# A trunk of three layers on one core: the second block's experts without a branch each, weights by slots, a Newton step on each reciprocal root

## The chip, the cores and the metric

One core of one Trainium2 chip runs the whole program. The metric is the device time of an execution in microseconds, the median of the runs. All data are 32-bit floats.

## The reference

The input is 256 tokens of 1024 features (x), and further 256 context tokens. Three layers follow each other. Each has a mixer over the tokens and a mixture of 16 experts, both behind a root-mean-square norm with a scale, a shift and a gate from a conditioning vector (adaLN).

```python
def first_block(...):                       # layers 0 and 1
    h = rms_norm(x, mix_norm_g[l]) * (1 + scale) + shift
    y = fourier_conv_mixer(h, ...) if l % 2 == 0 else windowed_attention(h, ...)
    x = x + gate * y
    h = rms_norm(x, ffn_norm_g[l]) * (1 + scale) + shift
    x = x + gate * ec_moe(h, router_w[l], ..., moe_w_gate[l], moe_w_up[l], moe_w_down[l])
```

In the first block the experts choose: each of the 16 takes the 32 tokens with the highest affinity, and has three matrices of 1024 x 1024 (gate, up, down). In the second block (layer 2) the tokens choose: of four groups of experts the best one, and in it the best two experts. An expert can get any number of tokens from 0 to 256; the mean is 32. Its matrices are w1 and w3 (1024 x 512) and w2 (512 x 1024), y = (silu(h w1) * (h w3)) w2, weighted by the token's gates. A last root-mean-square norm ends the program.

## The kernel before

**Weights.** All weights pass through a ring of 14 slots of 1 MB (`ring`, 128 partitions x 2048 floats). The list `order` says which slot holds what and in what order; class `Stream` asks for the next slot (L281, on SyncE's queue) as soon as a slot is freed in the program. Its order is adaLN weights, projections and experts as the layers need them: each expert of the first block is 12 slots (four each of gate, up, down), each of the second block 6 (two each of w1, w3, w2; 96 in all). A slot of a matrix is taken from the matrix as it lies in memory: `kview` puts row k * 128 + p on partition p, so a slot of gate, up, down or w2 is two runs of 4 KB in each partition, one of w1, w3 or a projection by columns (`by_cols`) four runs of 2 KB. The scale and shift part of an adaLN matrix is one run of 8 KB (of rows of 12 KB, or 24 KB in the second block), and a few tables (taps, transforms, pooling, `wb`) are laid out without gaps by the host.

**First block's experts** (`moe_ec`, matmuls of L1015): after the routing, expert by expert, gate, up and down on 32 tokens, with the results of four experts scattered back together (L1056).

**Second block's experts** (`moe2`): after the router, `rank` holds each token's place among its expert's tokens, `gates` its weights and `cnt` the number of tokens of each expert. `take` gathers the first 64 tokens of a pair of experts by a one-hot matmul (L1724) and prepares the way back (`sT`, L1739). `mlp` is one expert in steps: w1 and w3 (L1753, result in bank u), silu on ScalarE (L1758), the product `hid` on VectorE (L1762), its transposes (L1767), w2 (L1777) and the gated result Y (L1781). `scatter` adds a pair's Y back into x (L1685, L1686). Steps of two experts are interleaved. After w3 of every expert `more` (L1784) reads the expert's count into a register of TensorE, ScalarE and VectorE (L1786) and branches (L1787): with over 64 tokens the expert's weights are used again for slots 64 to 95 (`block`, matmuls on 32 tokens), with over 96 (L1797) and over 128 (L1799) for more. Only then are w1 and w3 freed. With the last scatter go the sums of squares for the last norm (L585) and the product with its weights (L1690).

**Roots.** `rstd` (L603 to L606) and three other places take a square root on ScalarE and a reciprocal on VectorE.

The order of instructions on each engine is made by a scheduling layer from the program's order and its own estimates of durations; a branch is a border that it moves little over.

Of the kernel before, what the change touches and what calls it, by code (L numbers as in the profile page):

```python
# [12 lines left out]
I32 = mybir.dt.int32  # L13
# [17 lines left out]
RING = 14  # L31


# ---------------------------------------------------------------- constants (shapes alone)
class Pack:
    """Columns of a [128, n] array, by name."""
# [95 lines left out]
def filter_consts():  # L132
    """Tables for the long filters."""
# [16 lines left out]
def tap_pack(i):  # L150
    """Tables for the spectrum of the 31 taps, the taps, and the bias of the convolution."""
# [15 lines left out]
def filter_pack(i):  # L167
    """Parameters of the long filters."""
# [19 lines left out]
def pool_consts():  # L188
    """Mean of a window less the middle, by the size of the window."""
# [63 lines left out]
# ---------------------------------------------------------------- the kernel  # L253
class Parts:
    """Feature tiles kept two by two, indexed as one [128, 2 * n, tokens]."""
# [8 lines left out]
class Stream:  # L264
    """Slots of weights, loaded in one order ahead of their use; parts of a slot lie side by side."""
# [6 lines left out]
    def pump(self):  # L272
        while self.issued < len(self.order) and self.issued - len(self.freed) < RING:
            key, parts = self.order[self.issued]
            t = self.pool.tile([128, SLOT], F32, name="w")
            v, at = t[:, :sum(int(np.prod(ap.shape[1:])) for ap in parts)], 0
            if len(parts[0].shape) == 3:
                v = v.rearrange("p (a b) -> p a b", a=parts[0].shape[1])
# [22 lines left out]
def weave(*gens):  # L301
    """Steps of several pieces of work in turn, each as (generator, steps at a time)."""
# [17 lines left out]
def trunk_kernel(ctx: ExitStack, tc: tile.TileContext, I: dict, O: dict):  # L320
# [16 lines left out]
    # ---- what stays  # L337
# [20 lines left out]
    def kview(ap, k0, k1):  # L358
        return ap[k0 * 128:k1 * 128].rearrange("(k p) n -> p k n", p=128)
# [1579 lines left out]
```

## Time and profile before

| | |
|---|---|
| median of the runs | 1871.93 us (3 runs, 1869.08 to 1872.28) |
| span of the profiled execution, first to last instruction | 1864.1 us |
| TensorE (matmul) busy | 1460.4 us, 78% |
| VectorE, ScalarE, GpSimd busy | 438.2, 238.4, 10.3 us |
| read from memory | 627.09 MB, 337 GB/s over the span |
| blocks for an expert's tokens past 64 that ran | 1 (L1753 with xgx: 128 records, two for a matmul, 64 matmuls a block) |

The runs are timed without the profile; the profiled execution's own time is its span. PE is TensorE, PEld its weight loads, DVE VectorE, ACT ScalarE, SP SyncE; a q behind a name is the engine's sequencer. PEclk is the share of TensorE's 2.4 GHz that was granted. A 32-bit matmul leaves two records. The DMA share is the mean busy share of the 16 DMA engines.

### The profile page before, as it was taken

The numbers are of one execution on the slowest core, as the hardware profiler recorded it, in microseconds if no ns is written. First come the engines' busy times: TensorE is split into PE (matmuls) and PEld (weight loads), VectorE is DVE, ScalarE is ACT, GpSimd is POOL, SyncE is SP. The second block draws the span as 40 slices with busy tenths as digits, with TensorE's granted clock in tenths as the row PEclk, the third lists the DMA queues.
The fourth block names the chain that finished last, engine by engine and source line by source line (L and its number), as shares of the span: only waits on it lengthen the run. The fifth ranks groups of instructions, "written<-read, shape, count | busy, mean of one in ns | idle before, by whom it ended". The sixth has DMA issues, their size and how long they took to land. (4 is left out here: it accounts for less than half of the span.)

```text
span 1864.1 us, 25272 instructions
## 1 busy us (share of the span) xinstructions
PE 1460.4 (78%) x10913; PEld 742.4 (40%) x10913; DVE 438.2 (24%) x981; ACT 238.4 (13%) x550; POOL 10.3 (1%) x19
## 2 busy tenths in 40 slices
PE   6997778767666699986676766677999978788887
PEld 2444324223222246452232322244767545445442
DVE  2513113110010057231110101101333241222123
ACT  2022002000000014221000000001222120001011
POOL 0000000000000000000000000000000000000000
PEclk9998868776676699996866866889989989999998
DMA  9987999999999998399999999999713748889770
GB/s 364 411 309 306 410 409 409 409 409 409 409 409 409 406 389 320 114 407 409 409 409 409 409 409 409 409 404 394 282 46 136 265 161 313 304 333 342 283 262 24
DMA packets 180860, 630.30 MB, mean 338 GB/s; under 512 B 10880, under 2 KB 13056, under 8 KB 174048
## 3 DMA queue, kind: packets, MB, share of 16 engines
q1 hardware_dynamic: 178464, 624.38, 86.1%
q0 software_dynamic: 1952, 3.16, 0.6%
q8 instruction: 117, 1.92, 0.4%
q10 hardware_dynamic: 288, 0.52, 0.1%
q14 instruction: 39, 0.32, 0.0%
HBM read 627.09 MB, written 1.05 MB: 337 GB/s over the span
## 5 line engine op out<-in xcount | busy, mean ns | idle before, releaser
L1015 PE MATMUL b<-w,xg 128*32 128x256 f32 x4096 | 361.6, 496 | 183.0 <-DMA w<-in_moe_w_up_dram 110.0
L1015 PEld LDWEIGHTS b<-w,xg 128*32 128x32 f32 x4096 | 136.3, 132 | 404.6 <-DMA w<-in_moe_w_up_dram 161.8
L1015 PE MATMUL b<-w,hidT 128*32 128x256 f32 x2048 | 185.5, 505 | 63.7 <-DMA w<-in_moe_w_down_dram 47.5
L1753 PE MATMUL u<-w,xg 128*64 128x256 f32 x1024 | 130.9, 399 | 14.7 <-PEq L1787 14.0
L1015 PEld LDWEIGHTS b<-w,hidT 128*32 128x32 f32 x2048 | 68.4, 135 | 165.3 <-DMA w<-in_moe_w_down_dram 88.3
L1035 DVE TENSOR_TENSOR hid<-b,sg 128x256 f32<-128x256 f32 x32 | 13.6, 425 | 512.6 <-PE b L1015 417.8
L1043 DVE SCALAR_TENSOR_TENSOR Y<-b,cc,gq 32x256 f32<-32x256 f32 x128 | 61.5, 481 | 223.9 <-PE b L1015 222.4
L1753 PEld LDWEIGHTS u<-w,xg 128*64 128x64 f32 x1024 | 82.0, 143 | 58.2 <-issue 29.8
L1777 PE MATMUL b<-w,hidT 128*64 128x512 f32 x256 | 73.5, 701 | 37.1 <-PEq L1787 33.2
L1030 ACT ACTIVATE sg<-b 128x256 f32<-128x256 f32 x32 | 12.3, 384 | 436.8 <-PE b L1015 436.7
L1777 PEld LDWEIGHTS b<-w,hidT 128*64 128x64 f32 x256 | 24.6, 161 | 76.8 <-issue 75.2
L1040 ACT COPY hidT<-b 128x256 f32<-128x256 f32 x32 | 11.9, 372 | 323.8 <-PE b L1038 323.8
L1056 PE MATMUL b<-Y,gT 128*128 128x512 f32 x64 | 39.1, 762 | 9.5 <-DVE Y L1043 9.5
L784 PE MATMUL b<-w,hT 128*128 128x512 f32 x96 | 43.3, 612 | 1.1 <-DVE hT L633 1.1
L461 DVE SCALAR_TENSOR_TENSOR w<-w,cond 128x1024 f32<-128x1024 f32 x35 | 43.5, 1277 | 1.2 <-DMA w<-in_ada_w_dram 1.1
L1137 PE MATMUL b<-w,hT 128*128 128x512 f32 x96 | 42.2, 594 | 0.0
L1762 DVE TENSOR_TENSOR hid<-u,sg 128x256 f32<-128x256 f32 x16 | 6.8, 425 | 147.9 <-PEq L1787 86.1
L952 PE MATMUL b<-oh,n 128*128 128x128 f32 x256 | 39.4, 320 | 0.9 <-DVE oh L995 0.9
L952 PEld LDWEIGHTS b<-oh,n 128*128 128x128 f32 x256 | 36.9, 231 | 7.5 <-issue 6.1
L1287 PE MATMUL b<-pe,w 128*128 128x256 f32 x160 | 38.6, 396 | 0.0
L1781 DVE TENSOR_TENSOR Y<-b,hkb 64x512 f32<-64x512 f32 x32 | 22.0, 689 | 67.7 <-PE b L1777 67.5
L1728 ACT ACTIVATE xg<-b,shsc 128x128 f32<-128x128 f32 x32 | 14.6, 460 | 158.5 <-DVE xg L1731 158.5
(445 smaller groups left out, 1484.7 us busy)
## 6 DMA issues: line engine op xcount, KB each, us to landing
w<-in_moe_w_gate_dram SPq DMA_DIRECT2D x128, 1024.0 KB, 18.5
w<-in_moe_w_up_dram SPq DMA_DIRECT2D x128, 1024.0 KB, 18.6
w<-in_moe_w_down_dram SPq DMA_DIRECT2D x128, 1024.0 KB, 18.5
w<-in_moe_w_dram SPq DMA_DIRECT2D x96, 1024.0 KB, 10.3
w<-in_ada_w_dram SPq DMA_DIRECT2D x72, 1024.0 KB, 13.1
w<-in_w_in_dram SPq DMA_DIRECT2D x8, 1024.0 KB, 16.6
w<-in_fc_w_in_dram SPq DMA_DIRECT2D x6, 1024.0 KB, 20.4
w<-in_attn_w_qkv_dram SPq DMA_DIRECT2D x6, 1024.0 KB, 16.1
```

The source lines that it names most:

```text
L461: V.scalar_tensor_tensor(into[:, hs], w[:, hs], c, into[:, hs], op0=OP.mult, op1=OP.add)
L784: T.matmul(p, hT[:, kt, b * 128:(b + 1) * 128], w(kt), start=kt == 0, stop=kt == 7)
L952: T.matmul(p[:, j * 128:(j + 1) * 128], n[:, b, dt * 128:(dt + 1) * 128], oh[:, b, g * 128:(g + 1) * 128], start=b == 0, stop=b == 1)
L1015: T.matmul(p[32 * q:32 * q + 32, :256], lhs(kt), w[:, k, q * 256:(q + 1) * 256], start=kt == 0, stop=kt == 7)
L1043: V.scalar_tensor_tensor(Y[32 * j:32 * j + 32, q * 256:(q + 1) * 256], pd[32 * q:32 * q + 32, :256], cc[32 * q:32 * q + 32, e:e + 1], gq[3 ...
L1056: T.matmul(p, gT[:, b * 128:(b + 1) * 128], Y[:, h * 512:(h + 1) * 512], start=True, stop=True)
L1137: T.matmul(p, hT[:, kt, b * 128:(b + 1) * 128], w(kt), start=kt == 0, stop=kt == 7)
L1287: T.matmul(p[:, j * 256:(j + 1) * 256], w(kt)[:, c0 + j * 128:c0 + (j + 1) * 128], h[:, kt], start=kt == 0, stop=kt == 7)
L1728: A.activation(xg[:, dt, :m], p[:, j * 128:j * 128 + m], AF.Identity, bias=shsc[:, 0, dt:dt + 1], scale=shsc[:, 1, dt:dt + 1])
L1753: T.matmul(p[rows[h], :nu], xg[:, kt, c], w(kt)[:, h * nu:(h + 1) * nu], start=kt == 0, stop=kt == 7)
L1777: T.matmul(pd[rows[h], :nd], hidT[:, kt % nj, rows[kt // nj]], w(kt)[:, h * nd:(h + 1) * nd], start=kt == 0, stop=kt == 3)
L1781: V.tensor_tensor(Y[c, h * nd:(h + 1) * nd], pd[rows[h], :nd], gq2[rows[h], at:at + nd], op=OP.mult)
```

## The change

1. **Layout.** The host cuts every matrix into slots (`weight_slots`): what goes into a slot lies in memory partition after partition, 8 KB each, and `Stream` loads it as one flat [128, 2048]. The bytes, the slots and their order stay.
2. **Second block.** `more` and its branches go. Every expert takes its first 64 tokens, and w1, w3 and w2 are freed right behind their last matmul. Tokens past 64 become jobs of 64 tokens: a list of at most seven (`keys`, `top`, `je`, `jk`, `ji`) is made on VectorE behind the routing, and behind the last pair's scatter a nest of branches runs as many jobs as there are, each with its expert's six slots loaded again on SyncE's queue from an address in a register, and its own gather, matmuls and scatter. The sums of the last norm stand behind the jobs.
3. **Roots.** After sqrt and reciprocal one Newton step, three small VectorE operations (`inv_root`), at all places.

Comments and docstrings are gone as well, so line numbers differ.

```diff
+def by_rows(w, per):
+    *lead, k, n = w.shape
+    w = w.reshape(*lead, k // (128 * per), per, 128, n)
+    return np.ascontiguousarray(np.swapaxes(w, -3, -2))
...
     def pump(self):
         while self.issued < len(self.order) and self.issued - len(self.freed) < RING:
-            key, parts = self.order[self.issued]
+            key, ap = self.order[self.issued]
             t = self.pool.tile([128, SLOT], F32, name="w")
...
-            for ap in parts:
-                n = ap.shape[-1]
-                self.nc.sync.dma_start(v[..., at:at + n], ap)
-                at += n
+            flat = ap.rearrange("p a b -> p (a b)") if len(ap.shape) == 3 else ap
+            v = t[:, :flat.shape[1]]
+            self.nc.sync.dma_start(v, flat)
...
+    def inv_root(m, n=2):
+        r = small.tile([128, 8], F32, name="root")[:, :n]
+        t = small.tile([128, 8], F32, name="step", bufs=1)[:, :n]
+        A.activation(r, m, AF.Sqrt)
+        V.reciprocal(r, r)
+        V.scalar_tensor_tensor(t, r, -0.5, r, op0=OP.mult, op1=OP.mult)
+        V.tensor_tensor(t, t, m, op=OP.mult)
+        V.scalar_tensor_tensor(r, t, 1.5, r, op0=OP.add, op1=OP.mult)
+        return r
...
-            def more(e, hid):
-                c = nc.values_load(cnt[0:1, e:e + 1], engines=ENGINES, min_val=0, max_val=256)
-                with tc.If(c > 64):
...
-                    block(64, 32)
-                    with tc.If(c > 96):
-                        block(96, 32)
-                        with tc.If(c > 128):
-                            block(128, 64)
-                            block(192, 64)
+            for k in range(3):
+                V.scalar_tensor_tensor(keys[:, k], cnt, 64.5 + 64 * k, cv("iota_r")[:, 256 - 48 + 16 * k:256 - 32 + 16 * k], op0=OP.is_gt, op1=OP.mult)
+            V.max(top, keys.rearrange("p k e -> p (k e)"))
+            V.tensor_scalar(at, top, 0.0, None, op0=OP.is_gt)
+            V.tensor_reduce(jk[:, 0:1], at, axis=AX.X, op=OP.add)
+            V.tensor_copy(ji[:, 8:9], jk[0:1, 0:1])
...
+            def job(j):
+                e = nc.values_load(ji[0:1, j:j + 1], engines=(mybir.EngineType.SP,), min_val=0, max_val=15, ...)
+                def load(nm):
+                    v = I[f"moe_{nm}_2"].rearrange("e i p k n -> p e i (k n)")
...
+                        nc.sync.dma_start(t, v[:, bass.ds(e, 1), i].rearrange("p e n -> p (e n)"))
...
+                take([(rs[:, 0], rs[:, 1])], t)
+                run(mlp(None, t["xg"], 0, t["Y"], lambda nm: ws[nm]))
+                scatter(t["sT"], t["Y"], 64)
+            def jobs(j=0):
+                if j == JOBS:
+                    return
+                with tc.If(n_jobs > j):
+                    job(j)
+                    jobs(j + 1)
...
-            scatter(t["sT"], t["Y"], 128, True)
+            scatter(t["sT"], t["Y"], 128)
+            jobs()
+            for b in range(2):
+                for h in range(2):
+                    hs = slice(h * 512, (h + 1) * 512)
+                    sums(ssf, b, h, x)
+                    (V if b else G).tensor_tensor(n[:, b, hs], x[:, b, hs], fg[:, hs], op=OP.mult)
             r = rstd(ssf)
```

The order of TensorE's instructions shows the second part. Before, from the branch behind expert 1's w3 to the one behind expert 2's; w1 and w3 of an expert are L1753, w2 L1777, the gather L1724, names with an x at the end belong to the block past 64 tokens:

```order
L1787 UNCONDITIONAL_BRANCH
L1753 MATMUL u<-w,xg 64x256 x13
L1777 MATMUL b<-w,hidT 64x512 x8
L1724 MATMUL b<-oh,n 128x128 x16
L1739 MATMUL b<-cst,ohg 128x128 x2
L1753 MATMUL u<-w,xg 64x256 x16
L1767 MATMUL b<-cst,hid 128x128 x2
L1753 MATMUL u<-w,xg 64x256 x3
L1786 TENSOR_LOAD cnt
L1787 COMPARE_AND_BRANCH
L1710 MATMUL b<-n,ohx 32x256 x8
```

Now, experts 8 and 9 on TensorE (w1 and w3 are L1769, w2 L1794, the transposes of hid L1784, scatter L1718, gather L1740):

```order
L1784 MATMUL b<-cst,hid 128x128 x2
L1794 MATMUL b<-w,hidT 64x512 x4
L1718 MATMUL b<-Y,sT 128x512 x2
L1794 MATMUL b<-w,hidT 64x512 x4
L1718 MATMUL b<-Y,sT 128x512 x2
L1769 MATMUL u<-w,xg 64x256 x8
L1740 MATMUL b<-oh,n 128x128 x3
L1769 MATMUL u<-w,xg 64x256 x8
L1740 MATMUL b<-oh,n 128x128 x6
```

Between two experts no load of a register and no branch is left, and from expert 6 on the transposes of hid stand directly ahead of the same expert's w2; before, part of the next expert's w3 stood between them.

SyncE's queue at the end, now (before, only branches around the last of the 96 slots and then the output stood there):

```order
L313 DMA w<-in_moe_w_2_dram 128x2048 x96
L1868 TENSOR_LOAD jobi
L1857 COMPARE_AND_BRANCH
L1827 TENSOR_LOAD jobi
L1836 ISA
L1836 DMA w<-in_moe_w_2_dram 128x2048
```

The number of jobs and the first job's expert are read behind the last of the 96 slots, and the job's six loads follow.

TensorE at the end, now; before, the program ended with a scatter, transposes, w2 and a scatter, with no branch behind the last expert's w3:

```order
L1718 MATMUL b<-Y,sT 128x512 x4
L1868 TENSOR_LOAD jobi
L1857 COMPARE_AND_BRANCH
L1740 MATMUL b<-oh,n 128x64 x16
L1755 MATMUL b<-cst,ohg 64x128 x2
L1769 MATMUL u<-w,xg 64x256 x32
L1784 MATMUL b<-cst,hid 128x128 x2
L1794 MATMUL b<-w,hidT 64x512 x8
L1718 MATMUL b<-Y,sT 128x512 x4
L1857 COMPARE_AND_BRANCH
```

A job's steps stand one behind the other with nothing between them, behind the last scatter, and a second branch follows each job.

## Rows read from the trace of the kernel before

**Rows 1.** The page's first line

```profile
span 1864.1 us, 25272 instructions
```

**Rows 2.** Windows: busy (x) of PE, PEld, DVE, ACT, POOL; PEclk, DMA share, GB/s

```profile
16.00:32.00 16.00, 16.00 (x69) 7.02 (x71) 3.51 (x6) 0.44 (x2) 0.00 (x0) 1.00 1.01 424
200.00:620.00 420.00, 297.47 (x2804) 116.26 (x2798) 63.95 (x125) 21.44 (x47) 0.00 (x0) 0.72 1.03 409
820.00:1280.00 460.00, 324.81 (x3214) 145.68 (x3206) 52.41 (x110) 29.48 (x65) 0.58 (x1) 0.76 1.03 408
1308.00:1314.00 6.00, 4.86 (x30) 3.25 (x31) 3.44 (x8) 3.99 (x5) 0.00 (x0) 0.53 1.04 386
1318.00:1324.00 6.00, 6.00 (x30) 5.28 (x29) 1.93 (x5) 0.00 (x0) 0.00 (x0) 1.00 1.03 421
1542.00:1842.00 300.00, 247.47 (x1685) 140.89 (x1681) 66.81 (x150) 26.86 (x69) 0.00 (x0) 0.92 0.76 280
```

**Rows 3.** Timeline of SyncE's queue: start, us, line, out<-in, count

```profile
182.51 2.96 SPq L281 DMA_DIRECT2D w<-in_moe_w_gate_dram  x4
...
623.51 11.85 SPq L281 DMA_DIRECT2D w<-in_moe_w_down_dram  x4
...
781.82 5.52 SPq L281 DMA_DIRECT2D w<-in_moe_w_gate_dram  x4
```

**Rows 4.** Waits of PE, 200 to 620: us, times, longest

```profile
PE b L1015 <- DMA w<-in_moe_w_up_dram: 52.0, 51, 2.6
```

**Rows 5.** Waits of PE, 1522 to 1864

```profile
PE b L1777 <- PEq L1787: 33.2, 8, 7.0
PE u L1753 <- PEq L1787: 14.0, 6, 3.9
...
PE b L1767 <- DVE hid L1762: 0.5, 1, 0.5
```

**Rows 6.** Line L1787 on PE's sequencer: ns min/median/max, first and last start

```profile
L1787 PEldq COMPARE_BRANCH  x16: 82/4794/6962, 1529.8 to 1832.9; - x16
```

**Rows 7.** Timeline of PE, 1610.5 to 1642: start, us, then idle before

```profile
1610.71 3.65 PE L1777 MATMUL b<-w,hidT 128*64 128x512 f32 x16 [2.20 <-DVE hid L1762]
1614.17 3.65 PE L1753 MATMUL u<-w,xg 128*64 128x256 f32 x32
1617.75 0.44 PE L1767 MATMUL b<-cst,hid 128*128 128x128 f32 x2
1618.12 3.67 PE L1753 MATMUL u<-w,xg 128*64 128x256 f32 x32
1628.82 5.50 PE L1777 MATMUL b<-w,hidT 128*64 128x512 f32 x16 [7.02 <-PEq L1787]
1634.24 3.70 PE L1685 MATMUL b<-Y,sT 128*128 128x512 f32 x8
1637.78 3.73 PE L1724 MATMUL b<-oh,n 128*128 128x128 f32 x32
...
1641.66 0.65 PE L1753 MATMUL u<-w,xg 128*64 128x256 f32 x4
```

**Rows 8.** Timeline of PE: the first gather; the block for one expert's further tokens

```profile
1522.54 5.82 PE L1724 MATMUL b<-oh,n 128*128 128x128 f32 x32 [2.05 <-DVE ohg L1735]
...
1803.79 1.07 PE L1710 MATMUL b<-n,ohx 128*32 128x256 f32 x16
...
1820.26 1.12 PE L1753 MATMUL u<-w,xg 128*64 128x256 f32 x4 [0.44 <-PEq L1797]
```

**Rows 9.** Timelines of PE, ACT and DVE at the end

```profile
1846.50 3.65 PE L1777 MATMUL b<-w,hidT 128*64 128x512 f32 x16 [0.52 <-ACT hidT L1769]
1850.94 3.79 PE L1685 MATMUL b<-Y,sT 128*128 128x512 f32 x8 [0.79 <-DVE Y L1781]
...
1856.55 0.60 ACT L585 ACTIVATE b<-x 128x512 f32<-128x512 f32 x1 [1.28 <-DVE x L1686]
...
1857.94 0.17 DVE L606 RECIPROCAL r<-r 128x2 f32<-128x2 f32 x1 [0.27 <-ACT r L605]
```

More of the change, by code (lines that the diff above doesn't have):

```diff
@@ L1679, in moe2, with scatter @@
             ssf = small.tile([128, 2, 2], F32, name="ss")
-            def scatter(sT, Y, k, last=False):
+            def scatter(sT, Y, k):
                 for b in range(2):
@@ L1707, in take @@
                     p = bank()
-                    for b in range(2):
-                        for q in range(4):
-                            T.matmul(p[32 * q:32 * q + 32, :256], oh[:, b, :32], n[:, b, q * 256:(q + 1) * 256], start=b == 0, stop=b == 1)
-                    A.copy(t["rows"], p[:, :256])
-                    p = bank()
-                    for j in range(2):
-                        T.transpose(p[:, j * 128:(j + 1) * 128], t["rows"][:, j * 128:(j + 1) * 128], ident)
-                    to = xg[:, :, :32].rearrange("p (q j) s -> p q j s", j=2)
@@ new lines, in take @@
+                    for j in range(4):
+                        dt = 4 * d4 + j
+                        for b in range(2):
+                            T.matmul(p[:, j * 128:j * 128 + m], n[:, b, dt * 128:(dt + 1) * 128], oh[:, b, :m], start=b == 0, stop=b == 1)
+                    for j in range(4):
+                        dt = 4 * d4 + j
+                        if j % 2:
+                            A.activation(xg[:, dt, :m], p[:, j * 128:j * 128 + m], AF.Identity,
+                                         bias=shsc[:, 0, dt:dt + 1], scale=shsc[:, 1, dt:dt + 1])
+                        else:
+                            V.tensor_scalar(xg[:, dt, :m], p[:, j * 128:j * 128 + m], shsc[:, 1, dt:dt + 1],
+                                            shsc[:, 0, dt:dt + 1], op0=OP.mult, op1=OP.add)
@@ L1751, in up @@
                     for kt in range(8):
-                        for h in range(parts):
-                            T.matmul(p[rows[h], :nu], xg[:, kt, c], w(kt)[:, h * nu:(h + 1) * nu], start=kt == 0, stop=kt == 7)
+                        for h in range(2):
+                            T.matmul(p[rows[h], :256], xg[:, kt, c], w[kt // 4][:, kt % 4, h * 256:(h + 1) * 256], start=kt == 0, stop=kt == 7)
+                    if get is None:
+                        free((nm, e), 2)
                     return p
@@ L1763, in mlp @@
+                V.tensor_tensor(hid, pu[:, :256], sg, op=OP.mult)
                 yield
                 pt = bank()
-                nj = nu // 128
-                for j in range(nj):
+                for j in range(2):
                     T.transpose(pt[:, j * 128:(j + 1) * 128], hid[:, j * 128:(j + 1) * 128], ident)
-                hidT = wk.tile([128, 2, 128], F32, name="hidT" + x, bufs=nb)
-                A.copy(hidT[:, :nj], pt[:, :nu])
-                if e == E - 1 and not x:
+                hidT = wk.tile([128, 2, 128], F32, name="hidT", bufs=2)
@@ L1771, in mlp @@
+                A.copy(hidT, pt[:, :256])
+                if e in (E - 1, None):
                     table_of_roots(hidT[0:1, 0, 0:1])
                 yield
-                w = rows_at(("w2", e), 2)
+                w = weights("w2")
                 pd = bank()
                 for kt in range(4):
-                    for h in range(parts):
-                        T.matmul(pd[rows[h], :nd], hidT[:, kt % nj, rows[kt // nj]], w(kt)[:, h * nd:(h + 1) * nd], start=kt == 0, stop=kt == 3)
+                    for h in range(2):
+                        T.matmul(pd[rows[h]], hidT[:, kt % 2, rows[kt // 2]], w[kt // 2][:, kt % 2, h * 512:(h + 1) * 512], start=kt == 0, stop=kt == 3)
@@ L1778, in mlp @@
+                if get is None:
+                    free(("w2", e), 2)
                 gq2 = gqs[2, 1]
[L1779 to L1781 removed]
+                for h in range(2):
+                    V.tensor_tensor(Y[c, h * 512:(h + 1) * 512], pd[rows[h]], gq2[rows[h]], op=OP.mult)
                 yield
[L1784 to L1801 removed]
```

245 lines of the change are left out of this document (122 added, 123 removed).

## The prediction, made before the changed kernel ran

> **What bounds the kernel now.** I read the span and the runs first, then the busy times by stretch, then who waited for whom in each stretch, and only then single instructions. The profiled execution spans 1864.1 us [rows 1]; the median of the runs, 1871.93, is 7.8 more. The sum below is made on the span, and 7.8 is carried over.
>
> The windows [rows 2] show two regimes. From 200 to 620 and from 820 to 1280 us (the experts of the first block's two layers) the DMA engines' share is 1.03, they move 409 and 408 GB/s, and TensorE holds only 0.72 and 0.76 of its clock. TensorE's waits there are for weights: for "up" alone 52.0 us in 51 waits [rows 4]. Whoever brings these slots sooner shortens the kernel one for one. From 1542 to 1842 (the second block's experts) the DMA share is 0.76 and TensorE is busy 247 of 300 us at 0.92 of the clock. There it waits for its own sequencer at the branch of L1787, 33.2 and 14.0 us [rows 5], and not for weights.
>
> **The weights by slots.** A slot of gate, up or down was two runs of 4 KB in each partition, a slot of w1 or w3 or of a projection four of 2 KB; now every slot is one run of 8 KB in each. Bytes and number of transfers stay. What long runs give is visible: at 16 to 32 us, when the 8 KB rows of ada_w land, 424 GB/s; at 1318 to 1324, when the table wb (6 KB rows) and the tables dft and pool (8 KB rows) land, 421; at 1308 to 1314, when 2 KB runs land, 386; with 4 KB runs 408 and 409 [rows 2]. wb, dft and pool lie in memory as the new slots will, partition after partition without a gap, so I take 421: a slot of 1048576 bytes takes 2.491 us instead of 2.564 (at 409), 0.073 less. From above I bound it by 424 (2.473, 0.091 less); from below by no gain at all, since the queue's engines are full at either run length.
>
> How many slots count: in layer 0 the 180 that are issued after the routing (first at 182.51, last four at 623.51), in layer 1 the 192 of the experts, the 6 of the projection loaded between and behind them, and the 4 gate slots that TensorE still waits for, 202 (first at 781.82) [rows 3]. 382 slots by 0.073 are 28 us, and the eight or so of them that had 2 KB runs (2.717 at 386) give 1 more: **29 us** less. In the mixers TensorE does not wait for weights, and I cost the new layout at nothing there: the cover is matmul work, and if it were gone the six slots of qkv would give 1 us.
>
> **The second block's experts without a branch each.** Before, TensorE's first gather starts at 1522.54 [rows 8] and the last sum into x ends at 1856.55, when ScalarE stops waiting for it [rows 9]: 334 us. What TensorE needs at full clock is read from one stretch [rows 7], start to start: w2 3.46 (1610.71 to 1614.17), w1 3.58 (to 1617.75), transposes 0.37 (to 1618.12), w3 again 3.58, 11.0 for an expert; scatter 3.54 (1634.24 to 1637.78), gather with its two transposes 3.88 (to 1641.66), 7.4 for a pair. Sixteen experts and eight pairs are 176 + 59 = 235 us. To this comes what the new order leaves open. From expert 6 on w2 stands right behind the transposes that it needs, ten times 0.52; in five of these the transposes stand right behind w3, 0.5 each [rows 5]; the last scatter waits 0.79 for Y (0.52 and 0.79 as at the end of the old program [rows 9]); and where 64-row and 128-row matmuls alternate I allow 8 us. That is 17. The first gather runs at low clock as now, 5.82 instead of 3.73, with the products behind it 4.5 in all. The list of jobs puts about eleven small VectorE operations of some 0.17 us (as RECIPROCAL, [rows 9]) between the routing and the first gather: 2. The last sum ends 1 after the last scatter. 235 + 17 + 4.5 + 2 + 1 = 260, so **74 us** less than 334.
>
> Where these go: 47 are the two lines of waits at the branch [rows 5], 16.5 the block for one expert's tokens past 64 (1803.79 to 1820.26 [rows 8]), and the rest is the clock, which falls after such a wait (7.02 us of waiting, and the w2 behind it takes 5.50 instead of 3.65 [rows 7]). What is late next is again TensorE, not DMA: a pair takes it 31 us, and 12 slots at 2.491 take 30, with 14 slots loaded before the first is used.
>
> **The job.** One block ran, so one expert has 65 to 96 tokens, and one job runs now, behind the 16 experts. Its weights are loaded a second time, 6 slots or 15 us; SP's order shows them behind the 96 slots with only a register load and a branch between, and a ring place is free once expert 13's w2 is done, some 30 us before the job. I cost them at nothing; without that cover it would be 15. SP's load of the number of jobs waits for the routing, but what stands behind it are the job's loads alone. The job is 64 slots wide where the block had 32, and nothing of another expert fills its waits. At full clock, step by step from [rows 5, 7, 9]: seven small operations of VectorE, a register load and the two one-hots, 2.5; the gather at most 3.7 (half its columns, but the same loads of tokens), 0.9 until the first gathered tokens are scaled; w1 and w3 7.2; hid 0.5, transposes 0.4, copy 0.5; w2 3.5; Y 0.8; scatter 3.5 and the last add 1: 24.5. Without the gather's half it is 22; with the whole at the clock of the first gather of now (5.82 for 3.73 [rows 7, 8]) it would be 34, of which I take half: 31. **25 us** more, between 22 and 31.
>
> **The tail.** The sums of squares no longer run between the last adds but behind the job's end: four instead of the last one, each 0.60 [rows 9] and some 0.2 to read the sum out, 2.5 more. They wait also for TensorE to pass over the other six jobs: the old branch took 0.08 to 6.96 us, 4.8 in the middle [rows 6]; with no transfers under way I take 3.4, of which the last add covers 1.8. The Newton step, three operations of 0.17 and their gaps, is 0.6. **5 us** more. The Newton step stands in four or five other places where all wait for it (layer 0's experts, mixer 1, twice in mixer 2, the second block's experts): **3 us** more. In layer 1's routing the DMA runs on and covers it.
>
> **Sum**: -29 - 74 + 25 + 5 + 3 = -70. 1864.1 - 70 = 1794 for the span, **1802 us** for the median.
>
> **Rivals.** *Run length gives nothing*: the 4 KB stretches already have a DMA share of 1.03, as have the long runs, so the engines may be at their limit by bytes. Against it stand 386, 409 and 421 GB/s in the order of the run lengths. Then 1802 + 29 = 1831 us. The Trainium skill (DMA: Bandwidth & Descriptors, Why small descriptors are slow (HBM only)) gives a fixed cost of some 3 cycles a packet beside one cycle for 32 bytes; as an estimate from that page, 8 KB for 4 KB would save 1.2%, or 12 us, and the sum would be 1819. The trace's step from 2 to 4 KB, 6%, is larger than that rule has it.
>
> *Slower: the gapless layout collides in memory.* All partitions' rows now lie 8 KB apart, a power of two, and 16 engines walk them in step; the ada_w rows that gave 424 lay 12 KB apart. If the slots came at the 386 GB/s of the 2 KB runs [rows 2], 374 of them would each take 0.153 longer, 57 more, where I have 29 less: 1802 + 86 = 1888, slower. It decides from about 392 GB/s (2.675 us, 0.11 by 374 slots, eats the 41 that the rest gives). Against it: wb, dft and pool, laid out so, at 421. [...]
>
> *The waits come back in the second block.* The 0.5 us waits from expert 6 on may lower the clock as the long ones do. If each costs what the one behind 7.02 us did, 1.85 [rows 7], ten give 18: 1820. For it: the window's 0.92. Against: the w2 behind 2.20 us of waiting took the full-speed 3.65 [rows 7].
>
> **How the numbers follow.** My forecast has 0.73, no gain by run length 0.12, the waits 0.10, the slower case 0.05. The stage without the 17 us of waits and the upper DMA rate give 1802 - 17 - 7 = 1778, and a short job 1772; no gain by run length gives 1831, with the job's upper bound or the waits 1837 to 1849, of which I leave the far part out: 1772 to 1834. A change within 0.2% (3.7 us, about what can be told from none) needs two cases to cancel: 0.01. Faster 0.94, slower 0.05.
>
> **What would show it.** Right: 418 to 424 GB/s in the two long stretches at the same share; no wait for a branch among the second block's experts, TensorE's clock there near 1.0, 31 to 33 us a pair; one job of some 25 us with no wait for its weights; three more small operations behind each root. Wrong: 409 or less in the long stretches; TensorE waiting for moe_w slots in the second block, or for the job's; more than one job; a tail of over 14 us behind the last add instead of 7.6.

## The result, and the profile after

The changed kernel takes 1795.55 us (median of 4 runs, 1795.07 to 1795.78) against 1870.51 of the kernel before (4 runs, 1869.02 to 1872.28): ratio 0.9592, 95% interval 0.9575 to 0.9609, so 75 us less. Compared once more (experiment 3) the ratio was 0.9594 (0.9570 to 0.9618). The span of the profiled execution fell from 1864.1 to 1793.9.

The page of the kernel after: the span, then TensorE's granted clock, the DMA share and the rate in 40 slices, and the packets. The clock has two levels, 1.2 and 2.4 GHz: a mean of 1.00 is the upper one throughout, a lower mean has stretches of the lower one in it.

```profile
span 1793.9 us, 25073 instructions
...
PEclk9997868878686689999687786789898998999998
DMA  9988899999999998379999999999931566999970
GB/s 371 420 313 320 350 421 421 421 421 421 421 421 421 420 412 339 131 306 408 420 421 421 420 421 420 421 421 421 420 125 47 196 239 240 422 420 413 386 303 25
DMA packets 89746, 636.00 MB, mean 355 GB/s; under 512 B 10944, under 2 KB 11072, under 8 KB 13344
```

The last of these lines in the page of the kernel before:

```profile
DMA packets 180860, 630.30 MB, mean 338 GB/s; under 512 B 10880, under 2 KB 13056, under 8 KB 174048
```

The packets follow the runs: nearly all had under 8 KB before, and few have now.

Windows of the kernel after; the columns are those of [rows 2].

```profile
200.00:620.00 420.00, 291.41 (x2907) 113.54 (x2906) 68.44 (x134) 22.35 (x49) 0.00 (x0) 0.77 1.01 421
820.00:1280.00 460.00, 319.13 (x3234) 143.91 (x3226) 56.48 (x120) 30.04 (x67) 0.58 (x1) 0.80 1.01 421
1522.00:1752.00 230.00, 220.98 (x1484) 122.17 (x1480) 65.05 (x142) 26.88 (x66) 0.00 (x0) 1.00 0.94 384
```

Beside [rows 2] the two long stretches go at 421 GB/s instead of 409 and 408, at a share of 1.01 instead of 1.03. The second block's window has TensorE busy 96% of it, at the full clock; before it was 247 of 300 us (82%) at 0.92.

Waits of TensorE from the first gather to the last pair's end, after (us in total, times, longest):

```profile
PE b L1794 <- ACT hidT L1786: 5.5, 10, 0.9
PE b L1784 <- DVE hid L1780: 2.9, 5, 0.6
PE b L1740 <- DVE jobat L1813: 1.4, 1, 1.4
PE b L1718 <- DVE Y L1799: 0.8, 1, 0.8
```

The waits for a branch, 33.2 and 14.0 us in [rows 5], are gone. What is left is the list that the prediction made from the order: w2 behind the transposes ten times, transposes behind w3 five times, the last scatter once. The 1.4 us behind `jobat`, a step of the list of jobs, stand ahead of the first gather, where 2.05 stood before [rows 8]: the list adds no wait there.

The table holds the stages of the profiled executions, in us. They are cut at instructions of the timelines: the first w-matmul of a layer's experts, the end of its last scatter, the first gather, the last sum into x (its end). The columns on the right belong to experiments below.

| stage | before | after | after, again | layout alone | second block alone | no Newton | no job | in order |
|---|---|---|---|---|---|---|---|---|
| start to layer 0's experts | 181.4 | 184.3 | 182.2 | 179.8 | 183.0 | 178.4 | 180.0 | 181.8 |
| layer 0's experts | 476.8 | 464.7 | 462.8 | 466.0 | 477.3 | 462.7 | 465.7 | 462.9 |
| mixer 1 and routing | 158.6 | 161.5 | 164.3 | 161.4 | 160.2 | 158.7 | 162.5 | 164.3 |
| layer 1's experts | 483.4 | 469.8 | 471.1 | 471.1 | 482.8 | 469.7 | 469.7 | 471.1 |
| mixer 2 and routing | 222.4 | 221.7 | 221.5 | 219.0 | 220.2 | 221.9 | 221.8 | 221.5 |
| second block's experts and job | 334.0 | 280.6 | 280.7 | 331.1 | 280.8 | 280.6 | 255.8 | 266.9 |
| last sum into x to the end | 7.6 | 11.3 | 11.1 | 7.7 | 10.4 | 10.4 | 8.1 | 11.1 |

The job and the end, in the timeline of the kernel after:

```profile
1757.96 5.72 PE L1740 MATMUL b<-oh,n 128*128 128x64 f32 x32 [2.06 <-DVE oh L1734]
1764.03 8.23 PE L1769 MATMUL u<-w,xg 128*64 128x256 f32 x64
...
1773.77 3.65 PE L1794 MATMUL b<-w,hidT 128*64 128x512 f32 x16 [0.46 <-ACT hidT L1786]
...
1778.21 3.70 PE L1718 MATMUL b<-Y,sT 64*128 64x512 f32 x8 [0.79 <-DVE Y L1799]
...
1781.94 0.69 DVE L1719 TENSOR_TENSOR x<-x,b 128x512 f32<-128x512 f32 x1 [0.17 <-PE b L1718]
1783.04 0.60 ACT L612 ACTIVATE b<-x 128x512 f32<-128x512 f32 x1 [7.81 <-PEq L1857]
...
1783.07 3.45 DVE L1891 TENSOR_TENSOR n<-x,fg 128x512 f32<-128x512 f32 x2 [0.44 <-PEq L1857]
...
1786.44 0.15 DVE L641 TENSOR_TENSOR r<-ss 128x2 f32<-128x2 f32 x1
...
1787.26 0.16 DVE L633 SCALAR_TENSOR_TENSOR step<-root 128x2 f32<-128x2 f32 x1
1787.46 0.16 DVE L634 TENSOR_TENSOR step<-step,r 128x2 f32<-128x2 f32 x1
1787.65 0.16 DVE L635 SCALAR_TENSOR_TENSOR root<-step,root 128x2 f32<-128x2 f32 x1
```

One job ran, and nowhere in it does TensorE wait for weights. It lasts from the end of the experts' last sum (near 1756.6) to 1782.63, 26 us. It begins slowly, with part of the gather and of w1 and w3 at the lower clock: the granted clock is 0.87 over the job. TensorE's branch over the other jobs, at the end:

```profile
L1857 PEldq COMPARE_BRANCH  x2: 196/2047/3898, 1778.9 to 1783.1; - x2
```

The long one starts at 1778.9, once the last scatter is issued, and ends at 1782.8: the scatter and the adds cover all but the 0.41 us between the last add (1782.63) and the sums (1783.04).

### The profile page after: what moved, and what is told of

It reads as the page before. It is cut to its first block, busy times and chain, and to the rows that moved or that the text cites. A ratio compares the mean times of both kernels' runs of the same rounds, so it can differ in the third digit from the quotient of the medians.

```text
span 1793.9 us, 25073 instructions
## 1 busy us (share of the span) xinstructions
PE 1423.3 (79%) x10848; PEld 727.8 (41%) x10848; DVE 446.9 (25%) x1034; ACT 242.5 (14%) x556; POOL 10.7 (1%) x19
## 3 DMA queue, kind: packets, MB, share of 16 engines
HBM read 633.38 MB, written 1.05 MB: 354 GB/s over the span
## 5 line engine op out<-in xcount | busy, mean ns | idle before, releaser
L1050 PE MATMUL b<-w,xg 128*32 128x256 f32 x4096 | 353.0, 486 | 183.3 <-DMA w<-in_moe_w_up_dram 104.1
L1050 PE MATMUL b<-w,hidT 128*32 128x256 f32 x2048 | 172.2, 472 | 67.8 <-DMA w<-in_moe_w_down_dram 51.6
L1070 DVE TENSOR_TENSOR hid<-b,sg 128x256 f32<-128x256 f32 x32 | 13.6, 425 | 502.2 <-PE b L1050 407.9
L1050 PEld LDWEIGHTS b<-w,hidT 128*32 128x32 f32 x2048 | 64.6, 129 | 162.9 <-DMA w<-in_moe_w_down_dram 91.9
L1769 PE MATMUL u<-w,xg 128*64 128x256 f32 x1088 | 128.3, 384 | 0.0
L1769 PEld LDWEIGHTS u<-w,xg 128*64 128x64 f32 x1088 | 78.4, 138 | 46.2 <-issue 10.5
L1794 PE MATMUL b<-w,hidT 128*64 128x512 f32 x272 | 65.8, 598 | 6.0 <-ACT hidT L1786 6.0
L1065 ACT ACTIVATE sg<-b 128x256 f32<-128x256 f32 x32 | 12.3, 384 | 426.0 <-PE b L1050 426.0
L1740 PE MATMUL b<-oh,n 128*128 128x128 f32 (+1 forms) x288 | 40.8, 301 | 3.5 <-DVE oh L1734 2.1
L1740 PEld LDWEIGHTS b<-oh,n 128*128 128x128 f32 x288 | 38.0, 212 | 11.3 <-issue 7.9
L1091 PE MATMUL b<-Y,gT 128*128 128x512 f32 x64 | 34.6, 683 | 9.5 <-DVE Y L1078 9.5
L987 PEld LDWEIGHTS b<-oh,n 128*128 128x128 f32 x256 | 36.6, 229 | 7.1 <-issue 5.7
L1718 PE MATMUL b<-Y,sT 128*128 128x512 f32 (+1 forms) x72 | 34.9, 614 | 1.6 <-DVE Y L1799 1.6
```

The source lines that it names most:

```text
L987: T.matmul(p[:, j * 128:(j + 1) * 128], n[:, b, dt * 128:(dt + 1) * 128], oh[:, b, g * 128:(g + 1) * 128], start=b == 0, stop=b == 1)
L1050: T.matmul(p[32 * q:32 * q + 32, :256], lhs(kt), w[:, k, q * 256:(q + 1) * 256], start=kt == 0, stop=kt == 7)
L1091: T.matmul(p, gT[:, b * 128:(b + 1) * 128], Y[:, h * 512:(h + 1) * 512], start=True, stop=True)
L1718: T.matmul(p, sT[:k, b * 128:(b + 1) * 128], Y[:k, h * 512:(h + 1) * 512], start=True, stop=True)
L1740: T.matmul(p[:, j * 128:j * 128 + m], n[:, b, dt * 128:(dt + 1) * 128], oh[:, b, :m], start=b == 0, stop=b == 1)
L1769: T.matmul(p[rows[h], :256], xg[:, kt, c], w[kt // 4][:, kt % 4, h * 256:(h + 1) * 256], start=kt == 0, stop=kt == 7)
```

## The experiments

Each kernel was compared with the kernel before on the same chip (median there 1868.32, 1869.29 and 1871.21 us in the three groups of runs). Between groups I compare ratios. A stage in the table above is that of one profiled execution.

### 1. The layout alone

```diff
+    a = {f"moe_w_{nm}": by_rows(i[f"moe_w_{nm}"], 2) for nm in ("gate", "up", "down")}
...
-                self.nc.sync.dma_start(v[..., at:at + n], ap)
+            self.nc.sync.dma_start(v, flat)
```

(against the kernel before: the first part of the change whole, for all matrices)

> The kernel before with the weights laid out by slots, and nothing else of the change: the second block's experts keep their branches, no root has a Newton step. My account (run length sets the rate, 0.073 us a slot): 420 GB/s in the two long stretches, some 13 us gained in each of layer 0's and layer 1's experts and 2 before them, so 28 to 30 us in all, 1841 us against 1870.5 of the kernel before; TensorE's clock between the root before layer 0's experts and their first weights stays as before (that stretch 25 us and not 30). Rival 1, three cycles a packet: 12 us, 1858. Rival 2, the low clock that the changed kernel shows in front of the experts comes from weights that land sooner, and not from the Newton step: the same stretches are slow here too, 8 us of the gain go, 1850.

Measured: 1836.89 us, ratio 0.9832 (0.9807 to 0.9857), 31 us less (27 to 36). The windows:

```profile
200.00:620.00 420.00, 291.67 (x2849) 113.98 (x2845) 65.65 (x128) 23.28 (x50) 0.00 (x0) 0.75 1.01 421
820.00:1270.00 450.00, 314.25 (x3159) 141.29 (x3161) 51.87 (x109) 29.15 (x64) 0.58 (x1) 0.78 1.01 421
```

The rate is that of the changed kernel, and the table has 10.8 and 12.3 us less in the two layers' experts. 12 us for the whole would have been the three cycles a packet; it is not that. As for rival 2, the stretch from the root to layer 0's first weights takes 23.6 us (156.15 to 179.79) and is not slow in this profile; mixer 1 is 2.8 longer than before (161.4). The second block gains 2.9 and keeps its waits for the branch:

```profile
PE b L1806 <- PEq L1816: 32.5, 8, 6.9
PE u L1782 <- PEq L1816: 11.2, 6, 3.4
```

### 2. The second block alone

```diff
-            self.nc.sync.dma_start(v, flat)
+                self.nc.sync.dma_start(v[..., at:at + n], ap)
...
-                    v = I[f"moe_{nm}_2"].rearrange("e i p k n -> p e i (k n)")
+                    v = I[f"moe_{nm}_2"][0].rearrange("e (i k p) n -> p e i k n", i=2, p=128)
...
-        V.scalar_tensor_tensor(r, t, 1.5, r, op0=OP.add, op1=OP.mult)
```

(against the changed kernel: layout and Newton step, all three operations, taken back, the second block left as changed)

> The kernel before with the rewritten second block alone (no branch for each expert, one list of jobs behind them), with the weights in memory as before and no Newton step. My account: everything up to the first gather as before (1522.5 us), from there to the last sum into x some 281 instead of 334, the tail 3 longer: 50 us less, 1820. Rival: without the long runs a pair's 12 slots take 8 x 2.717 + 4 x 2.564 = 32 us, more than TensorE's 29 to 32.7, so weights become the wait there: up to 8 us of the gain go, 1828, with waits for moe_w1_2 to moe_w3_2 in the stage.

Measured: 1815.41 us, ratio 0.9713 (0.9693 to 0.9732), 54 us less (50 to 57). The stage takes 280.8 us, as with the long runs. The windows of layer 0 and of the second block:

```profile
200.00:620.00 420.00, 289.92 (x2820) 112.23 (x2812) 65.47 (x128) 21.84 (x48) 0.00 (x0) 0.75 1.03 409
1560.00:1760.00 200.00, 192.68 (x1275) 106.17 (x1272) 57.12 (x123) 21.82 (x55) 0.00 (x0) 1.00 1.04 394
```

The DMA engines are full there (1.04), yet TensorE has no wait for weights in this stage. So the rival falls; that the slots loaded ahead cover the difference is how I read it. Experiments 1 and 2 add up to 85 us; 2.9 of the first lie in a stage whose time the second sets, so 82, and the whole change gave 75. The Newton step is in neither.

### 3. No Newton step, and the clock ahead of layer 0's experts

```diff
-        V.scalar_tensor_tensor(t, r, -0.5, r, op0=OP.mult, op1=OP.mult)
-        V.tensor_tensor(t, t, m, op=OP.mult)
-        V.scalar_tensor_tensor(r, t, 1.5, r, op0=OP.add, op1=OP.mult)
```

> The changed kernel without the Newton step on the roots (their last digits differ). My account: the step's 0.6 us each, and with it the low clock in front of layer 0's experts and of mixer 1, where the changed kernel lost 5.0 and 3.1 us: 8 to 10 us less, 1786; the stretch from the root to the first weights of layer 0's experts back from 28.5 to 23.5 us. Rival: the low clock there has nothing to do with the step; then only the five places by 0.6, 3 to 4 us, 1792.

Measured: 1784.86 us, ratio 0.9560 (0.9540 to 0.9580), against 0.9594 (0.9570 to 0.9618) of the changed kernel beside other runs: 6 us, with an interval of about 0 to 12. In the table the profile without the step is shorter up to layer 0's experts (178.4), in mixer 1 (158.7) and at the end (10.4 for 11.1 or 11.3). Mixer 1 can't be put down to the step: the layout alone, which has no step, takes 161.4 there.

The first profile had spent 5.0 us more than the kernel before between the root and layer 0's first weights, and there the transposes and the router's matmuls ran at a low clock. I had put that down to the step: the wait ahead of the transposes grew from 0.49 to 1.20. So the changed kernel ran again, and once with the step left out at this place alone.

> The changed kernel once more, for a second profile and as the base of the three beside it: 1795 us. In the first profile the stretch from the root before layer 0's experts to their first weights took 28.5 us, against 23.5 before the change and 24.1 in the run without jobs, which has the Newton step as well. If the step's wait lowers the clock there, 28.5 comes again; if the low clock there varies from one execution to the next, 24 to 29, whatever the step.

```diff
-            scale_rows(n, x, rstd(ss))
+            scale_rows(n, x, rstd(ss, l > 0))
```

> The changed kernel with the root before layer 0's experts left without its Newton step (its last digits differ). If the step's wait lowers the clock there: 5 us less than the changed kernel beside it. If the step costs its own 0.5 us there and the clock varies: within 2 us of it.

Measured: 1795.16 us for the changed kernel, 1795.44 without the step there, ratios 0.9594 and 0.9597. First the timeline of TensorE in the first profile of the changed kernel, then in the second:

```profile
157.69 2.81 PE L679 MATMUL b<-cst,n 128*128 128x128 f32 x16 [1.20 <-DVE n L646]
160.29 3.43 PE L940 MATMUL b<-vec,shsc 128*128 128x16 f32 x16
```

```profile
160.05 1.97 PE L679 MATMUL b<-cst,n 128*128 128x128 f32 x16 [1.20 <-DVE n L646]
161.85 1.86 PE L940 MATMUL b<-vec,shsc 128*128 128x16 f32 x16
```

The same program with the same wait of 1.20 us took 6.24 us for the two once and 3.83 the other time; over 155.5 to 163.5 us the granted clock was 0.70 and 1.00. The low clock there comes and goes from one execution to the next, and without the step there the time is the same (1795.44 for 1795.16). The idea that the step's wait causes it falls, and with it "8 to 10 us" for the step; that the time without any step came out near the 1786 that was expected is luck. What the step costs beyond its own 0.6 us a place is not settled within these intervals, and no run shows what brings the low clock about there.

### 4. No job

```diff
             scatter(t["sT"], t["Y"], 128)
-            jobs()
```

> The changed kernel without the jobs: tokens past the first 64 of an expert are left out, the list of jobs is still made. My account: the job takes 26 us from the last add of the experts to its own last add, and the branch behind it 0.4: 1769. Rival 1, the job's six loads slowed the last experts: 2 to 4 less still, 1766. Rival 2, TensorE's branch over the other six jobs (3.9 us in the profile, beside the last scatter) costs by itself: 1766 also, but then the experts' stage is as long as before and the tail 3 shorter.

Measured: 1768.62 us, ratio 0.9465 (0.9446 to 0.9484), 24 us under the changed kernel by ratio. From the first gather to the end of the last pair's scatter the experts take 253.9 us with and without the jobs, so the job's loads do not slow the experts, and rival 1 falls. The stage shrinks from 280.6 to 255.8, so the job adds 24.8 to it; that is 1.2 less than its own 26, since without it the last add ends 1.9 us behind the scatter and not 0.7. The end shrinks as well, from 11.3 to 8.1: without a branch behind the scatter the sums stand between the adds again, and VectorE's products too. With the job there, the sums are over by 1785.6 and the root still waits until 1786.44, for the two products of L1891 (3.45 us) that stand ahead of it on VectorE. TensorE's branch holds the sums up for the 0.41 us given above, and the longer end is mostly work that can no longer stand between the adds; so rival 2 falls too.

### 5. What a branch costs: a short and a long one

```diff
+            def branch(e):
+                c = nc.values_load(ci[0:1, e:e + 1], engines=(mybir.EngineType.PE,), min_val=0, max_val=256)
+                with tc.If(c > 255):
+                    p = bank()
+                    for _ in range(4):
+                        T.transpose(p[:, :128], ident, ident)
...
                 next(cur, 0)
+                if e < E:
+                    branch(e)
                 next(prev, 0)
```

(320 in place of 4 for the long one)

> The changed kernel with a branch for each expert put back on TensorE alone, at its old place behind w3, over 4 transposes that never run. Theory J, the old price was the jump over some 300 instructions that are not at hand: a jump this short costs at most 0.5 us, 16 by 0.5, up to 8 us, 1795 to 1803. Rival B, any branch holds TensorE up until what stands before it is done and refetched: 16 by 4.8 as before, partly covered, 50 us more, 1845. Rival O, the branch only keeps the scheduler from moving work across it: the stage changes with the order, 10 us either way.

> The same with 320 transposes in the branch that never run. Theory J: the old price comes back, 47 us of waits and with them the low clock, the stage some 55 us longer, 1850. Rivals B and O: the same time as the short one.

Measured: 1803.21 us (ratio 0.9631, 0.9606 to 0.9655) with the short one, 1908.85 (1.0194, 1.0167 to 1.0222) with the long one. The stage takes 287.9 and 392.1 us instead of 280.7. The branch's line on TensorE's sequencer (ns: least, middle, most), first short, then long:

```profile
L1867 PEldq COMPARE_BRANCH  x16: 202/207/247, 1505.6 to 1737.6; - x16
```

```profile
L1867 PEldq COMPARE_BRANCH  x16: 3741/5968/6531, 1506.7 to 1838.7; - x16
```

Neither body ever runs; the two kernels differ in how far TensorE jumps. A short jump takes 0.21 us, a long one 6.0, and [rows 6] with 4.8 in the middle is of the long kind. So theory J holds, and rival B falls. Of the 7.2 us that the short branches add to the stage sixteen jumps are 3.4; the rest is not explained, and rival O, the branch as a border for the scheduler, may have its part in it. For the long branches J's sum of 1850 was too low: the sixteen jumps last 93 us together, and 77 of the 111 us leave TensorE idle under these names (of the DMA more below):

```profile
PE b L1784 <- PEq L1867: 45.3, 8, 6.4
PE b L1794 <- DMA w<-in_moe_w_dram: 23.8, 5, 5.2
PE u L1769 <- PEq L1867: 6.6, 2, 3.5
```

Beside them the granted clock is 0.86 from 1522 to 1850:

```profile
1522.00:1850.00 328.00, 242.89 (x1413) 127.99 (x1414) 60.06 (x134) 24.94 (x63) 0.00 (x0) 0.86 0.72 274
```

Why the branches of the kernel before, 74 us of jumps in all, left only 47 us of waits, no run shows. What happens in the jump can be seen on the queue that loads instructions (its packets, MB and share of the engines), in the page of the kernel after, of the short and of the long one:

```profile
q8 instruction: 87, 1.43, 0.3%
```

```profile
q8 instruction: 88, 1.44, 0.3%
```

```profile
q8 instruction: 120, 1.97, 0.4%
```

Sixteen long jumps load 33 blocks of some 16 KB more, two each; sixteen short ones load 1. The kernel before had 117. The times at which the trace has these blocks fit: within each of the sixteen long jumps a block lands, and the jump ends 1.35 to 1.57 us behind it (behind the later one, where there are two); within the short jumps none lands. In the kernel before a block lands within each of the fifteen jumps of 3.4 to 7.0 us, and none within the branch of 0.08. What fills the time before the block is asked for is not shown. The Trainium skill (Runtime: NRT & Kernel Launch, Instruction fetch mechanics) says that a taken branch to code outside the window that is at hand has to fetch it before the engine goes on; the trace agrees, and the price here is 6.0 us.

In the long kernel's list of waits 23.8 us carry the name of a DMA. One of them, in its timeline:

```profile
1605.15 3.67 PE L1769 MATMUL u<-w,xg 128*64 128x256 f32 x32
1613.51 5.35 PE L1794 MATMUL b<-w,hidT 128*64 128x512 f32 x16 [4.68 <-DMA w<-in_moe_w_dram]
```

A branch of this kernel runs from 1606.9 for 5.99 us, to the semaphore at 1613.0: the gap is the jump, whatever name stands behind it. The other four of these waits end 0.6 us behind a branch as well.

### 6. TensorE's order held as written

```diff
+    def in_order(ins):
+        return tc.keep_in_program_order(ins) if pin else ins
...
-                    T.transpose(pt[:, j * 128:(j + 1) * 128], hid[:, j * 128:(j + 1) * 128], ident)
+                    in_order(T.transpose(pt[:, j * 128:(j + 1) * 128], hid[:, j * 128:(j + 1) * 128], ident))
```

(and so for all matmuls and transposes of the experts behind the first gather, up to the last scatter)

> The changed kernel with TensorE's instructions in the second block's experts held in the order in which the program is written: transposes of an expert, w3 of the next, then its w2. My account: of the 254.5 us from the first gather to the last scatter of the experts, 11 are the waits of w2 for the transposed product and of the transposes for it, which this order covers; 244 to 247, 1786 for the whole. Rival: the weights are as late as TensorE there (DMA share 1.01 up to 1633 us), so waits for moe_w1_2 to moe_w2_2 take the place of these: 254 again, 1795.

Measured: 1779.52 us, ratio 0.9509 (0.9482 to 0.9537), 16 less than the changed kernel by either, where 9 were expected. The stage falls by 13.8, and the waits in it to these:

```profile
PE b L1723 <- DVE Y L1804: 0.8, 1, 0.8
PE b L1799 <- ACT hidT L1791: 0.5, 1, 0.5
```

The stage holds two things that moved apart. From the first gather to the last add of the experts it is 239.2 us and not 254.6, so the order gives 15.4 there; 8 of them are the waits of w2 and of the transposes. The other 7 fit the alternation of 64-row and 128-row matmuls, for which the prediction had allowed 8 and which this order hardly has; no run changed that alone. The job, whose order was not held, took 27.7 us in this profile and 26.0 in that of the changed kernel, at a granted clock of 0.81 and 0.87. No wait for weights took the place of the others, though the DMA share is 1.01 up to 1700 us here, as it was to 1633.

### 7. Shorter and longer runs

```diff
-    a = {f"moe_w_{nm}": by_rows(i[f"moe_w_{nm}"], 2) for nm in ("gate", "up", "down")}
+    a = {f"moe_w_{nm}": by_runs(i[f"moe_w_{nm}"]) for nm in ("gate", "up", "down")}
...
+                self.nc.sync.dma_start(t.rearrange("p (c n) -> p c n", n=RUN), ap.rearrange("c p n -> p c n"))
```

> The changed kernel with the slots of gate, up and down in runs of 2 KB in each partition (four parts of a slot behind each other in memory, each without a gap), all else as changed. My account (a fixed 9.5 ns a run): 386 GB/s in the two long stretches, 372 slots by 0.226 us, 84 us longer, 1879, slower than the kernel before. Rival 1, a fixed cost of three cycles a packet: 3.4% of a slot, 32 us, 1827. Rival 2, what slowed the 2 KB stretch at 1308 us of the kernel before was the mix of transfers there and not the run length: under 10 us.

```diff
-RING = 14
+RING = 7
...
-    a = {f"moe_w_{nm}": by_rows(i[f"moe_w_{nm}"], 2) for nm in ("gate", "up", "down")}
+    a = {f"moe_w_{nm}": by_rows(i[f"moe_w_{nm}"], 4) for nm in ("gate", "up", "down")}
...
+            t = self.pool.tile([128, WIDE], F32, name="w")
```

> The changed kernel with two neighbouring slots of gate, up and down in one transfer, one run of 16 KB in each partition, ring of 7 places of 16 KB. From 2, 4 and 8 KB at 386, 409 and 421 GB/s one engine takes 84.9, 160.2 and 311.4 ns a run, which is 9.5 ns and 37.7 ns a KB, so 16 KB would go at 427: 372 slots by 0.035 us, 13 less, 1782, if the fixed part is paid by the run. Rival: a run is cut into pieces of at most 8 KB or less, or the rate has its limit at 421: the same time, or some us longer through places that come free two by two.

Measured: 1877.82 us with 2 KB (ratio 1.0032, 1.0018 to 1.0046), 1789.94 with 16 KB (0.9581, 0.9557 to 0.9606), 5 less than the changed kernel beside it, which the intervals don't tell from none. The windows of layer 0, first 2 KB, then 16 KB:

```profile
200.00:620.00 420.00, 295.63 (x2638) 111.31 (x2626) 63.32 (x123) 20.66 (x45) 0.00 (x0) 0.67 1.05 386
```

```profile
200.00:620.00 420.00, 260.02 (x2876) 122.65 (x2876) 65.41 (x128) 23.10 (x50) 0.00 (x0) 0.84 1.01 427
```

The rates came out as worked out beforehand, 386 and 427 GB/s: a run costs one engine 9.5 ns and 37.7 ns a KB. The 386 came again with the large matrices, so the mix of transfers at 1308 us (rival 2) was not its reason; 427 is the forecast of a length that had not been measured. With 2 KB the two layers take 504.4 and 513.6 us, 84 more than the second profile of the changed kernel, as expected. With 16 KB they give 0.4 and 4.1 instead of 13: the rate is there, but in layer 0 the first expert's last transfer finds no free place and is issued near 184 us instead of 157, two slots or 5 us behind. Seven wide places are a coarser ring than fourteen; no run changed the ring alone. The profile with 16 KB is that of the fastest of its five runs, so its stages are to be read with care.

The Trainium skill (DMA: Bandwidth & Descriptors, Why small descriptors are slow (HBM only)) has about 3 cycles fixed for each packet, beside one cycle for each beat of 32 bytes. As an estimate from that, 2 KB would have cost 32 us; the traces show 84, 2.6 times that. The Trainium skill's ceiling of 435 GB/s (DMA: Bandwidth & Descriptors, Where 436 GB/s comes from) agrees with what the two costs above give for very long runs, as an estimate: 37.7 ns a KB on 16 engines is 435.

### 8. Both: the order held, and 16 KB for all experts

```diff
-    a["moe_w1_2"], a["moe_w3_2"] = (by_rows(i[f"moe_{nm}_2"][0], 4) for nm in ("w1", "w3"))
-    a["moe_w2_2"] = by_rows(i["moe_w2_2"][0], 2)
+    a["moe_w1_2"], a["moe_w3_2"] = (by_rows(i[f"moe_{nm}_2"][0], 8) for nm in ("w1", "w3"))
+    a["moe_w2_2"] = by_rows(i["moe_w2_2"][0], 4)
```

(on top of 6 and of the 16 KB of 7)

> The changed kernel with TensorE's order in the second block held as written and all experts' weights in transfers of 16 KB runs, the second block's too, ring of 7 places of 16 KB. My account: 13.8 us from the order, as measured alone, 5 from the longer runs, and the second block no longer loses the 3 us that it lost with 8 KB transfers in a shared place: 1773. Rival: TensorE in order is held by the weights once places come free two by two: 1780, as the order alone.

Measured: 1768.85 us, ratio 0.9446 (0.9426 to 0.9467), about 28 us under the changed kernel by ratio and 26 by the medians. That is below both forecasts, 1773 and 1780. The second block's stage is 261.7 us, 5.2 less than with the order alone, and TensorE has no gap from 1500 to 1700:

```profile
1500.00:1600.00 100.00, 100.00 (x751) 59.46 (x751) 28.95 (x77) 14.62 (x35) 0.00 (x0) 1.00 0.95 402
1600.00:1700.00 100.00, 100.00 (x692) 58.21 (x690) 32.51 (x69) 12.70 (x32) 0.00 (x0) 1.00 1.01 427
```

Little of the 5.2 us is won where the weights are waited for: the experts take 238.9 us, and with the order alone it was 239.2. 4.9 lie in the job, whose windows follow, of experiment 6, of this one and of the 16 KB of 7:

```profile
1740.74:1768.39 27.65, 23.74 (x124) 14.75 (x124) 7.61 (x22) 5.18 (x10) 0.00 (x0) 0.81 0.01 1
1733.48:1756.24 22.76, 18.85 (x124) 10.84 (x124) 7.61 (x21) 5.18 (x10) 0.00 (x0) 1.00 0.01 2
1742.83:1771.43 28.60, 24.69 (x124) 14.71 (x124) 7.61 (x21) 5.18 (x10) 0.00 (x0) 0.77 0.01 2
```

The same job takes 22.8 us at a granted clock of 1.00, 26.0 at 0.87 and 28.6 at 0.77. In all of these its gather follows the same wait of 2.06 us, so that wait alone does not decide the clock. Of the 3 us that the second block lost in the profile of 7 with 16 KB, 2.6 lie in the job as well; the expectation above had put them down to the ring's shared places. Another 5.5 of the 12.4 us between the two spans (1779.5 and 1767.1) lie in mixer 1 (158.8 for 164.3). Why the clock and mixer 1 differ is open; each of these kernels has one profile.

## Why the prediction was right, and where not

**The whole.** 1802 was forecast, 1772 to 1834; it is 1795.55. The sum made on the span was 1794, and the span is 1793.9, closer than its terms deserve: they are off by up to 5 us each, in both directions, and the profiled execution of the kernel before was a short one (next paragraph). That much of the agreement is luck: by the medians the change gave 75 us, where 70 were forecast. Two bounds do not follow from their own terms: half of the way from 24.5 to 34 is 29 for the job, not 31, and 1778 less the 3 us of a short job is 1775, not 1772. Neither touches the forecast.

**"7.8 is carried over".** This step is the miss in the median. The profiled execution of the changed kernel took 1795.63 as a run, 1.7 more than its span, and the later runs, those of the kernel before among them, show 1.7 to 2.2. So the profiled execution of the kernel before was a run of about 1866, six below the median, and not one with 7.8 us outside its span. Later runs of that kernel spread from 1863 to 1877. Which stage is longer in the longer ones no profile shows.

**The weights by slots, -29.** Measured -31 alone (27 to 36). 421 was taken and 421 came; by the table the experts of the two layers give 12.1 and 13.6 and the start to the root ahead of layer 0's experts 2.1 (157.84 to 155.74), 27.8. In the second profile of the changed kernel the experts give 14.0 and 12.3, and the root stands at 158.10, so the 2.1 do not come in every execution. The rival *run length gives nothing* is out, with the 12 us estimated beside it, and so is the collision: with rows 8 KB apart the rate was 421.

**The second block's experts, -74.** The stage without the job is 255.8 instead of 334.0: -78.2. No branch waits, clock 1.00. The list of jobs, allowed 2, hides where VectorE's one-hots made TensorE wait already; the low clock at the first gather cost 2.4 rather than 4.5: the gather took 6.15 us for 3.73, the products behind it their full-speed 10.58. The waits that the order leaves were there as listed, 9.2 us of them, and the clock stayed at 1.00; the rival *the waits come back* is out. *Late next is again TensorE*: shown by experiment 2, where slower weights changed nothing.

**The job, +25.** 24.8, weights hidden: SyncE issued them from 1721.40, 36 us ahead. The number fits better than its steps: they were summed at full clock to 24.5, where the job of experiment 8 took 22.8 at a granted clock of 1.00, and the 26.0 of the changed kernel hold some 3 us of low clock.

**The tail, +5.** 3.7. The sums are as sized, and the branch (3.9 for 3.4) is covered but for 0.41 us; the 0.85 us behind VectorE's products were not seen.

**Newton elsewhere, +3.** With the 0.6 in the tail 3.6 were forecast, and 6 (0 to 12) measured. The stretches between the stages are 7.2 longer in the first profile: 5.0 at the one place where the clock was low in that execution, and 2.9 in mixer 1, which is as much longer in the layout alone, without the step (mixer 2 is 0.7 shorter). So beyond the step's own 0.6 us a place no run shows a price.

## What to carry to other kernels

A branch that is never taken into its body still makes TensorE jump over that body, and here a jump over hundreds of instructions cost it some 6 us: put rare work behind one branch at the end, or keep what is jumped over short. Where DMA engines are full, as in the first block here (a share of 1.01 to 1.05), lay weights out so that each partition's share of a transfer is one run; from two measured run lengths the fixed and the variable cost follow, and they forecast the next length, though a coarser ring can take the gain back. When a scheduler's order leaves small waits in a long stretch, holding the order as written is a cheap trial.

## What was not expected

The price of 6.0 us for a jump against 0.21 for a short one, with two blocks of 16 KB reloaded for each, was larger than the 47 us of waits in [rows 5] suggested: 16 long jumps made the stage 111 us longer. And the granted clock in one and the same stretch of one program was 0.70 in one execution and 1.00 in the next, which moved the stretch by 4.4 us (28.5 and 24.1) while the spans were 1793.9 and 1793.7: a few us in one stage of a single profile say little. The job shows the same at its own place, with 22.8 to 28.6 us for the same instructions.
